# Mamba-2 and latent attention on one core: where the first maxima, the output weight's low halves and the last low halves are computed

## The chip, the cores and the metric

The kernel runs on one core of a Trainium2 chip. The metric is the device time of one execution in microseconds (us); three executions were timed, and one execution was recorded by the hardware profiler. The engines are TensorE (PE in the profile, with its weight loads as PEld), VectorE (DVE), ScalarE (ACT), GpSimd (POOL) and SyncE (SP), which here only issues DMAs. The granted clock is the share of its full speed that TensorE was allowed in a stretch of the trace.

## The reference

Two layers over 2048 tokens of 1024 channels: a Mamba-2 mixer, then multi-head latent attention with 16 heads. The change lies in the second layer:

```python
def causal_block_attention(q_nope, q_rope, k_nope, k_rope, v):
    scale = (QK_NOPE + QK_ROPE) ** -0.5          # 64 + 32
    ...
    s = (q_nope . k_nope + q_rope . k_rope) * scale
    p = softmax(where(mask, s, -inf))
    return p @ v

def mla_mixer(h, k_nope, k_rope, v, cos, sin, w_in, g_q, w_uq, w_out):
    cq, gate = split(h @ w_in, [384])
    q = (rms_norm(cq, g_q) @ w_uq).reshape(..., 16, 64 + 32)
    ...
    o = causal_block_attention(q_nope, q_rope, k_nope, k_rope, v)
    o = o.reshape(..., 1024) * silu(gate)
    return o @ w_out
```

The result is `h + mla_mixer(...)`, followed by a last RMS norm. Every product is made to nearly float32 precision: an operand is split into a high half and a low half (high = the value rounded to a short type, low = value minus high), and three products high·high, high·low, low·high are added in PSUM.

## The kernel before, in words

**Stages.** Tokens go in four blocks of TB = 512. After the Mamba-2 layer, `mla` runs over the blocks b = 0 to 3: the latent key and value, the query's latent, then two gate sweeps (`mla_gate(b, 0)` and `mla_gate(b, 1)`), each of which multiplies eight 128-channel pieces of the input with four 128-column pieces of the gate weight, in eight steps of twelve products (L84 to L86, three for each pair of halves). Between the steps `mla` calls a few items of `mla_up`: keys (groups 0 and 1), values (2 and 3), the query's rotary part (6) and the query (4 and 5). The driver asks for two items a step in sweep 0 and one a step in sweep 1. An item's result is split by ScalarE and VectorE (`pair16`, L115 and L116) and written to DRAM by GpSimd's DMA queue. A gate result is emptied from its PSUM bank by ScalarE (tanh, L1081) and VectorE (product, L1082).

**PSUM.** Eight banks of 128x512 float32: four under the tag "mm" and four under "tr". Gate sweep 0 holds "mm" and sweep 1 holds "tr"; key and value items use "tr", query items "mm". In attention, six banks are called "s" (scores and maxima) and two "o".

**Attention.** `heads` treats 64 jobs (16 heads by four query blocks). For each job it first needs the maximum of each row of scores. This is made in chunks of up to 512 keys: a product (L1239) and a VectorE reduction (L1242), whose second operand, the `fence`, masks the keys that a query does not see. When a job's last chunk is done, the maxima are copied to float16 by ScalarE (L1248), the remainder is subtracted by GpSimd (L1249), VectorE transposes both (L1251), and a DMA through `m_d` puts them into two extra rows of the query tile. Job n's scores can then be made with the maximum already subtracted: `scores` (L1258) handles a *duo*, two tiles of 128 keys by 512 queries, with three products for each tile (and a mask on the diagonal), ScalarE's exponential (L1276) and copy to the high half (L1281). The low half of the probabilities (`lows`, L1291, tile `PTs`) is a subtraction by GpSimd in two pieces of 512 columns for full duos, and by VectorE for diagonal duos, in one piece, one duo later. `values` (L1306 to L1308) multiplies a duo's probabilities with the values some duos later. There are 320 duos.

**What sets the order.** Each engine works through its own queue in the order in which the program is written; PE's order in attention is written by hand. The list `due` says how far the maxima must have come at each duo; `some(...)` makes chunks up to a point, four times in a duo. Ahead of the first duo, `some(due[0])` makes 31 chunks: the 24 of jobs 0 to 2 and 7 of job 3. In some 16 duos at the end no maxima are left to make.

**The output weight.** While attention ends, `back` has already begun in the queues: its `weights(k)` splits eight 128x1024 pieces of the output weight, the high half by ScalarE (L1408), the low half by GpSimd (L1409). Pieces 2 to 5 go to tiles `W` (some 70 us ahead of attention's end), pieces 0, 1 into the first key tile `K0`, and pieces 6, 7 into the second, `K1`, which is free only when attention is done. The back stage multiplies by pieces 0 to 7 in turn.

**Tiles.** `xT` holds the eight pieces of a block's input (high and low half side by side), later the query tiles of attention; `K0` and `K1` hold keys and values of two heads, with room left behind them.

## Time and profile before

| | |
|---|---|
| median of 3 runs | 2934.28 us (2931.23 to 2935.17) |
| the profiled execution | 2936.12 us, of which its span is 2934.3 us |
| mean granted clock of TensorE | 0.987 |
| TensorE busy | 97% of the span |
| VectorE, ScalarE, GpSimd busy | 71%, 62%, 30% |
| DMA | 441.30 MB, mean 150 GB/s |

The profile page and the trace's views give times in us from the start of the span. A row of a timeline reads: start, duration, engine, line of the kernel, operation, output <- inputs, shapes and types, a count if several lie side by side, and in brackets the idle time of that engine just before, with what ended it. A row of a group gives the number of instructions, their busy time, and the mean in ns of one. The last block's gate sweeps and projections end at 1997 us (first chunk of maxima); attention goes from there to about 2747; the back stage follows.

### The profile page before, as it was taken

The numbers are of one execution on the slowest core, as the hardware profiler recorded it, in microseconds if no ns is written. First come the engines' busy times: TensorE is split into PE (matmuls) and PEld (weight loads), VectorE is DVE, ScalarE is ACT, GpSimd is POOL, SyncE is SP. The second block draws the span as 40 slices with busy tenths as digits, with TensorE's granted clock in tenths as the row PEclk, the third lists the DMA queues.
The fourth block names the chain that finished last, engine by engine and source line by source line (L and its number), as shares of the span: only waits on it lengthen the run. The fifth ranks groups of instructions, "written<-read, shape, count | busy, mean of one in ns | idle before, by whom it ended". The sixth has DMA issues, their size and how long they took to land. (4 is left out here: it accounts for less than half of the span.)

```text
span 2934.3 us, 58650 instructions
## 1 busy us (share of the span) xinstructions
PE 2844.8 (97%) x21582; PEld 1670.0 (57%) x21582; DVE 2096.4 (71%) x5050; ACT 1830.4 (62%) x3976; POOL 874.8 (30%) x993
## 2 busy tenths in 40 slices
PE   7899999999999999999999999998999999998998
PEld 3456556555555555554565545544666666665787
DVE  6789887887777778788775554346777777776354
ACT  8777655666666666556553433234888888887512
POOL 0212221221212212122211121222665665666300
PEclk9999999999999999999999999998999999999999
DMA  8765535445474445636446655561212223222452
GB/s 285 253 203 190 170 119 208 156 141 168 134 243 141 139 160 192 225 126 202 137 152 217 200 186 177 183 200 54 69 49 70 63 52 73 66 66 84 161 198 108
DMA packets 244755, 441.30 MB, mean 150 GB/s; under 512 B 69842, under 2 KB 111506, under 8 KB 243028
## 3 DMA queue, kind: packets, MB, share of 16 engines
q1 hardware_dynamic: 233332, 401.64, 43.0%
q0 software_dynamic: 11136, 35.92, 3.4%
q8 instruction: 169, 2.77, 0.4%
q14 instruction: 118, 0.97, 0.1%
HBM read 332.73 MB, written 104.73 MB: 149 GB/s over the span
## 5 line engine op out<-in xcount | busy, mean ns | idle before, releaser
L1291 POOL TENSOR_TENSOR PTs<-x,PTs 128x512 f16<-128x512 f32 x384 | 437.5, 1163 | 248.3 <-ACT PTs L1281 163.9
L1276 ACT ACTIVATE x<-s 128x512 f32<-128x512 f32 (+3 forms) x640 | 327.4, 525 | 56.4 <-PE s L1272 36.2
L84 PE MATMUL mm<-xT,wsp 128*128 128x512 f16 x800 | 305.8, 382 | 8.3 <-ACT wsp L115 6.1
L85 PE MATMUL mm<-xT,wsp 128*128 128x512 f16 x800 | 304.9, 381 | 0.0
L86 PE MATMUL mm<-xT,wsp 128*128 128x512 f16 x800 | 304.1, 381 | 0.0
L1281 ACT ACTIVATE PTs<-x 128x1024 f16<-128x1024 f32 (+1 forms) x320 | 297.1, 928 | 9.4
L1242 DVE CUSTOM_DVE_ANT_0 junk<-s,fence,mx 128x512 bf16<-128x512 f32 (+3 forms) x384 | 249.5, 650 | 46.9 <-PE s L1239 4.1
L1308 PE MATMUL o<-K,PTs 128*128 128x65 f16 x2176 | 263.2, 193 | 7.6 <-POOL PTs L1291 7.0
L1306 PE MATMUL o<-K,PTs 128*128 128x64 f16 x2176 | 264.6, 192 | 0.0
L1307 PE MATMUL o<-K,PTs 128*128 128x65 f16 x2176 | 264.3, 194 | 0.0
L802 POOL TENSOR_TENSOR Xp<-Xw,Xp 128x512 fp32r<-128x512 f32 x64 | 89.5, 1398 | 501.0 <-ACT Xp L801 300.8
L1239 PE MATMUL s<-K,xT 96*128 96x512 f16 (+3 forms) x640 | 225.8, 356 | 12.4 <-DVE mx L1242 10.8
L1306 PEld LDWEIGHTS <-PTs 128*128 128x128 f16 x2176 | 204.9, 97 | 52.3 <-issue 4.7
L85 PE MATMUL mm<-wsp,xT 128*128 128x512 f16 (+1 forms) x640 | 231.0, 361 | 3.2 <-DVE wsp L116 3.2
L84 PE MATMUL mm<-wsp,xT 128*128 128x512 f16 (+1 forms) x640 | 231.0, 362 | 2.9 <-ACT craw L606 2.6
L1307 PEld LDWEIGHTS <-PTs 128*128 128x128 f16 x2176 | 203.1, 97 | 53.5 <-issue 1.1
L612 DVE SCALAR_TENSOR_TENSOR cacc<-craw,pack,cacc 128x512 f32<-128x512 f32 x288 | 216.3, 779 | 23.9 <-ACT cacc L610 23.0
L86 PE MATMUL mm<-wsp,xT 128*128 128x512 f16 (+1 forms) x640 | 231.3, 362 | 0.0
L1270 PE MATMUL s<-xT,K 98*128 98x512 f16 (+3 forms) x640 | 224.9, 351 | 4.0 <-DVE mx L1242 4.0
L1271 PE MATMUL s<-xT,K 96*128 96x512 f16 (+3 forms) x640 | 224.6, 351 | 0.0
L1272 PE MATMUL s<-xT,K 96*128 96x512 f16 (+3 forms) x640 | 222.8, 348 | 0.0
L1308 PEld LDWEIGHTS <-PTs 128*128 128x128 f16 x2176 | 201.9, 98 | 8.6 <-POOL PTs L1291 8.1
(458 smaller groups left out, 7219.3 us busy)
## 6 DMA issues: line engine op xcount, KB each, us to landing
wsp<-wi_d SPq DMA_DIRECT2D x96, 512.0 KB
big<-cumT SPq DMA_DIRECT2D x64, 512.0 KB
wraw<-in_ssm_w_out_dram SPq DMA_DIRECT2D x96, 256.0 KB
wi_d<-wsp SPq DMA_DIRECT2D x32, 512.0 KB
wsp<-wo_d SPq DMA_DIRECT2D x32, 512.0 KB
wsp<-wu_d SPq DMA_DIRECT2D x28, 512.0 KB
hx<-in_ssm_w_in_dram SPq DMA_DIRECT2D x48, 256.0 KB
wraw<-in_ssm_w_in_dram SPq DMA_DIRECT2D x48, 256.0 KB
```

Of the source, the lines that this page charges most:

```text
L84: mm(out, l_hi, r_hi, start=start, stop=False)
L85: mm(out, l_hi, r_lo, start=False, stop=False)
L86: mm(out, l_lo, r_hi, start=False, stop=stop)
L1239: mm(s[:, :w], Q[0:96, 0, qs], K[0:96, 0, c0:c0 + w], start=True, stop=True)
L1242: v.tensor_tensor_reduce(junk[:, :w], s[:, :w], fence[:, at:at + w], -1.0 / MSCALE, peak[n][:, i - 1, j:j + 1] if i else 3.0e38, ALU.add, ...
L1270: mm(s, K[0:98, 0, ks], Q[0:98, 0, c], start=True, stop=False)
L1276: act(o, s, AF.Exp)
L1281: act(u[:, 0, at:end], x[:, at:end], AF.Copy)
L1291: engine.tensor_tensor(u[:, 1, a:b], x[:, a:b], u[:, 0, a:b], ALU.subtract)
L1306: mm(o[:, 0:64], hi, V[:, k, 0:64], start=k == 0 and j == 0, stop=False, skip_group_check=True)
L1307: mm(o[:, 0:65], hi, V[:, k, 64:129], start=False, stop=False, skip_group_check=True)
L1308: mm(o[:, 0:65], lo, V[:, k, 64:129], start=False, stop=k == 4 * qb + j, skip_group_check=True)
```

## The change

Three things move. First, the chunks of jobs 0, 1 and 2 are made by a new generator, `first_maxima`, three after each step of the last block's second gate sweep, in the "mm" banks. For that, all items of `mla_up` of the last block are issued with the first sweep (three a step, the rest at its end); the first two query tiles get a place behind the keys and values in `K0` and `K1`, filled as soon as blocks 0 and 1 are known; a third, of the high half alone, gets an "xs" tile. `heads` builds a fence of its own again, and its loop starts with 24 chunks made, and without the call ahead of the first duo. Second, `weights(k)` has VectorE make the low half. Third, once all chunks are made, a duo's low half is cut at column 512: VectorE makes the columns below, GpSimd those above, both at once.

The core of the diff (helpers `cuts`, `raise_fence`, `peaks`, `turn_peaks` and `rows` hold the code that stood in `heads`):

```diff
@@ mla @@
-                go(up, 2)
+                go(up, 3 if last else 2)
...
             go(cq)
+            if last:
+                go(up)
...
-            after = iter(()) if last else self.prep(NB + b + 1, None, "mm", 1)
+            after = self.first_maxima() if last else self.prep(NB + b + 1, None, "mm", 1)
             for n in range(8):
                 go(main, 1)
                 go(up, 1)
-                if not last:
-                    go(after, 1)
-                elif n == 2:
+                go(after, 3 if last else 1)
+                if last and n == 0:
                     self.load_vq()
@@ open_heads, load_vq, load_q @@
+            at = 2 * T + T // P * 130
+            Q = self.quer[0, i] = kv[i][0:98, at:at + 2 * TB].rearrange("p (s t) -> p s t", s=2)
+            self.fill_q(Q, 0, i)
...
         self.load_k(0, NB - 1, NB)
-        self.load_q(0, 0)
         self.load_v(0)
-        self.load_q(0, 1)
...
+    def first_maxima(self):
+        nc = self.nc
+        late, misc = (self.t(self.sp, "xs", [P, 2, TB], BF16, bufs=8) for _ in range(2))
+        Q2, junk = late[0:96, 0].bitcast(F16), late[:, 1]
+        misc = misc.rearrange("p s t -> p (s t)")
+        fence = self.raise_fence(misc[:, 0:TB + P])
...
+        nc.gpsimd.memset(turned, 0.0)
+        ts = slice(2 * TB, 3 * TB)
+        nc.sync.dma_start(Q2[0:64], self.qn_d[0:64, 0, ts])
+        nc.sync.dma_start(Q2[64:80], self.q1_d[0:16, 0, ts])
+        nc.sync.dma_start(Q2[80:96], self.q2_d[0:16, 0, ts])
+        K = self.keys[0]
+        for n in range(3):
+            Q = Q2 if n == 2 else self.quer[0, n][:, 0]
+            for j in range(4):
+                parts = self.cuts(n, j)
+                for i, (c0, w) in enumerate(parts):
+                    s = self.t(self.pp, "mm", [P, TB], bufs=4)
+                    self.peaks(s, Q[:, j * P:(j + 1) * P], K[:, 0, c0:c0 + w], fence, junk, peak[:, n], i, j,
+                               i == len(parts) - 1)
+                    if j < 3 or i < len(parts) - 1:
+                        yield
+            self.turn_peaks(n, peak[:, n, n], turned[:, 32 * n:32 * n + 32], rT[:, 32 * n:32 * n + 32])
+            if n < 2:
+                self.rows(n, self.quer[0, n])
+            yield
@@ heads @@
-        fence = self.t(sp, "fence", [P, TB + P], BF16, bufs=1)
-        nc.gpsimd.memset(fence[:, :TB], -LIFT)
-        nc.gpsimd.tensor_scalar(fence[:, TB:], self.mk, -LIFT, None, ALU.add)
...
+        fence = self.raise_fence(self.t(sp, "fence", [P, TB + P], BF16, bufs=1))
+        for n in range(2, 5):
+            self.load_q(n // NB, n % NB)
+        self.rows(2, quer[0, 2])
...
-            if kb < 4 * qb:
+            if made == len(chunks):
+                lows(u, x, at, TB, v)
+                lows(u, x, TB, end, nc.gpsimd)
+            elif kb < 4 * qb:
                 lows(u, x, at, end, nc.gpsimd)
             else:
                 fresh.append((u, x, at, end, v))
...
-            cut = [at, TB, end] if engine is nc.gpsimd else [at, end]
+            cut = [at, TB, end] if engine is nc.gpsimd and at < TB else [at, end]
...
-        step, later, held, fresh, made = [0], [], [], [], 0
+        step, later, held, fresh, made = [0], [], [], [], ends[2]
...
-        some(due[0])
@@ back, weights @@
-                nc.gpsimd.tensor_tensor(lo, self.wraw[k], hi.bitcast(F32), ALU.subtract)
+                v.tensor_tensor(lo, self.wraw[k], hi.bitcast(F32), ALU.subtract)
```

How the instructions stand on the engines, at three places. On PE, at the end of the last sweep: before, the last product of a query item (into `mm`) is followed by the first chunk's product (`s`, keys times the query tile `xT`):

```order
L86 MATMUL mm_21633<-yT_21103,wsp_21436 128x512
L1239 LDWEIGHTS xT_21454
L1239 MATMUL s_21680<-K_3813_20590,xT_21454 128x128
L1239 LDWEIGHTS xT_21454
L1239 MATMUL s_21684<-K_3813_20590,xT_21454 128x256
L1239 LDWEIGHTS xT_21454
```

Now the same chunks (L1213, into `mm` banks, query and keys both in the key tile) stand between the first two steps' products of the sweep (`tr`):

```order
L85 MATMUL tr_21511<-xT_20319,Xd_21519 128x512
L86 LDWEIGHTS Xd_21519
L86 MATMUL tr_21511<-xT_20319,Xd_21519 128x512
L1213 LDWEIGHTS K_3813_20590
L1213 MATMUL mm_21538<-K_3813_20590 128x128
L1213 LDWEIGHTS K_3813_20590
L1213 MATMUL mm_21541<-K_3813_20590 128x256
L1213 LDWEIGHTS K_3813_20590
L1213 MATMUL mm_21544<-K_3813_20590 128x384
L84 LDWEIGHTS y_21514
L84 MATMUL tr_21512<-xT_20261,y_21514 128x512
```

What moved: the chunks, from behind the sweep into it, three a step. On GpSimd, at the start of attention, before: the last stores of query items, three memsets, the fence, and then the subtractions for jobs 0 to 2:

```order
L1104 DMA qn_d<-Xp_21643 256x1x512
L1198 MEMSET nm_4003_21663 128x32
L1198 MEMSET nm_4004_21664 128x32
L1198 MEMSET nm_4005_21665 128x32
L1201 MEMSET fence_21669 128x512
L1202 TENSOR_SCALAR fence_21669<-mk 128x128
L1249 TENSOR_TENSOR nm_4003_21663<-mx_21675,nm_4003_21663 128x4
L1249 TENSOR_TENSOR nm_4004_21664<-mx_21703,nm_4004_21664 128x4
```

Now the three subtractions (L1223, in an `xs` tile) come first, and `heads`' memsets and its fence (which the 25th chunk reads) behind them:

```order
L1105 DMA qn_d<-big_21506 256x1x512
L1223 TENSOR_TENSOR xs_21531<-xs_21531 128x4 x3
L1271 MEMSET nm_4027_21757 128x32
L1271 MEMSET nm_4028_21758 128x32
L1271 MEMSET nm_4029_21759 128x32
L1206 MEMSET fence_21763 128x512
L1207 TENSOR_SCALAR fence_21763<-mk 128x128
L1350 TENSOR_TENSOR PTs_21852<-x_21851,PTs_21852 128x512 x2
```

What moved: the subtractions, ahead of the fence. On GpSimd some 70 us ahead of attention's end, before: three of the weight pieces (`W`) between the low halves of probabilities (`PTs`) and a subtraction for maxima (`nm`):

```order
L1291 TENSOR_TENSOR PTs_35556<-x_35555,PTs_35556 128x512 x2
L1409 TENSOR_TENSOR W_37173<-wr_35496,W_37173 128x2x512
L1291 TENSOR_TENSOR PTs_35612<-x_35611,PTs_35612 128x512 x2
L1409 TENSOR_TENSOR W_37209<-wr_37067,W_37209 128x2x512
L1291 TENSOR_TENSOR PTs_35652<-x_35651,PTs_35652 128x512 x2
L1249 TENSOR_TENSOR nm_4004_21664<-mx_35593,nm_4004_21664 128x4
L1409 TENSOR_TENSOR W_37243<-wr_37102,W_37243 128x2x512
```

Now the same pieces stand on VectorE, between the reductions of chunks (L1215), a head's result (`Op`) and a gating product of the back stage (`xT`, L1482):

```order
L1384 TENSOR_TENSOR Op_35621<-o_35431,ri_35619 128x4x64
L1467 TENSOR_TENSOR W_37155<-wr_35472,W_37155 128x2x512
L1215 ISA junk_35634,mx_35569<-s_35635,fence_21763 128x512
L1215 ISA mx_35569 128x1
L1482 SCALAR_TENSOR_TENSOR xT_37086<-xT_37086,us_37036 128x512
L1215 ISA junk_35659,mx_35569<-s_35660,fence_21763,mx_35569 128x384
L1215 ISA mx_35569 128x1
L1467 TENSOR_TENSOR W_37191<-wr_37049,W_37191 128x2x512
```

What moved: the weight pieces, from GpSimd's queue into VectorE's.

## The prediction

> **What bounds the kernel now.** I read the page first, then the windows around the places that the change touches, then the engines' timelines there.

> ```profile
> span 2934.3 us, 58650 instructions
> PE 2844.8 (97%) x21582; PEld 1670.0 (57%) x21582; DVE 2096.4 (71%) x5050; ACT 1830.4 (62%) x3976; POOL 874.8 (30%) x993
> PEclk9999999999999999999999999998999999999999
> ```

> TensorE (PE) is busy for 97% of the span, and its products are the same before and after. So only time in which PE stands idle, or runs under a lowered clock, can be won. The clock row has one dip, in slice 28, where attention starts. The windows (columns: time and length, busy us of PE, its weight loads, DVE, ACT, POOL, then granted clock, DMA share, GB/s) show the dips:

> ```profile
> 1976.00:1997.00 21.00, 21.00 (x99) 9.56 (x98) 7.25 (x10) 6.22 (x10) 3.38 (x5) 1.00 0.43 146
> 2000.00:2010.00 10.00, 6.01 (x12) 1.25 (x12) 7.37 (x26) 0.41 (x2) 1.19 (x4) 0.50 0.08 27
> 2010.00:2020.00 10.00, 6.49 (x13) 1.25 (x12) 8.38 (x26) 0.20 (x1) 0.38 (x2) 0.50 0.01 2
> 2020.00:2030.00 10.00, 9.42 (x51) 4.65 (x50) 8.01 (x24) 5.38 (x10) 0.02 (x1) 0.64 0.09 23
> 2660.00:2670.00 10.00, 7.39 (x89) 4.49 (x87) 8.70 (x25) 8.64 (x14) 8.10 (x7) 1.00 0.49 164
> 2670.00:2680.00 10.00, 6.04 (x63) 3.44 (x64) 4.64 (x9) 6.54 (x12) 10.00 (x8) 0.79 0.30 101
> 2680.00:2690.00 10.00, 10.00 (x84) 5.40 (x83) 7.94 (x22) 5.68 (x8) 5.50 (x6) 0.70 0.15 54
> 2735.00:2740.00 5.00, 5.00 (x74) 3.46 (x73) 0.00 (x0) 4.94 (x7) 5.00 (x5) 1.00 0.02 3
> ```

> In the last gate sweep (first row) PE is full and VectorE (DVE) only a third busy. Behind it, for some 24 us, VectorE sets the pace with the first maxima, and PE's clock falls to half. Around 2670 us GpSimd (POOL) is full; at the end of attention (last row) VectorE idles while GpSimd and ScalarE (ACT) are full. The change's three parts aim at these three places.

> **Part a, the first maxima in the gate sweep.** PE's timeline (start, duration) gives the sweep's step, its end, the first scores and the clock's return:

> ```profile
> 1988.69 0.38 PE L84 MATMUL tr<-xT,st 128*128 128x512 f16 x1
> 1991.28 0.38 PE L84 MATMUL mm<-yT,wsp 128*128 128x512 f16 x1
> 1997.11 0.22 PE L1239 MATMUL s<-K,xT 96*128 96x128 f16 x1
> 2021.25 0.59 PE L1270 MATMUL s<-xT,K 98*128 98x512 f16 x1 [0.32 <-DVE mx L1242]
> 2027.17 0.41 PE L1271 MATMUL s<-xT,K 96*128 96x512 f16 x1
> ```

> Twelve products of 512 columns, one step, take 1991.28 − 1988.69 = 2.59 us, 0.216 each; eight steps take 20.7. All up-projections now stand ahead of this sweep. PE was full up to 1997.11 and does the same work, so the sweep starts at 1997.11 − 20.7 = 1976.4, plus 0.9 for two query projections that wait in sweep 0 for a PSUM bank still being emptied: 1977.3. (Emptying takes 1.8: a product's 0.38 and a bit, tanh and its VectorE product at 0.69 each, rows below. A query projection has nine products, 1.94 us, so one of them between two uses of a bank covers it. By the order that stands for nearly all; two stand closer, and I estimate 0.2 and 0.7.) The 24 chunks laced in, blocks 0, 1 and 2 of head 0, hold 1280 + 3328 + 5376 = 9984 columns: 9984/512 × 0.216 = 4.2 us of PE. So PE leaves the sweep at 1977.3 + 20.7 + 4.2 = 2002.2, instead of reaching the first scores at 2021.25.

> VectorE does not follow that fast. ACT's tanh and VectorE's rows (brackets: idle time before it, and what ended it):

> ```profile
> 1944.21 0.69 ACT L1081 ACTIVATE xs<-mm,mdown 128x512 f32<-128x512 f32 x1 [0.70 <-PE mm L86]
> ```

> ```profile
> 1944.93 0.69 DVE L1082 SCALAR_TENSOR_TENSOR xs<-xs,mm 128x512 f32<-128x512 f32 x1 [0.69 <-ACT xs L1081]
> 2001.02 0.29 DVE L1242 CUSTOM_DVE_ANT_0 junk<-s,fence 128x128 bf16<-128x128 f32 x1 [2.24 <-POOL fence L1202]
> 2018.69 0.75 DVE L1242 CUSTOM_DVE_ANT_0 junk<-s,fence,mx 128x512 bf16<-128x512 f32 x1
> 2019.59 0.69 DVE L1242 CUSTOM_DVE_ANT_0 junk<-s,fence 128x512 bf16<-128x512 f32 x1
> ```

> The row at 2019.59 is the 25th chunk; the 24 ahead of it took 2019.59 − 2001.02 = 18.57 us. In the sweep, with four gate evacuations of 0.69 among them, VectorE needs about 21.3 us if nothing stops it; three chunks a step, in steps that are now 2.59 + 0.5 long, spread them over 25, and the last ones, the widest, come at the sweep's end together with the evacuations. I set the last chunk's end at 1977.3 + 28.9 = 2006.2: PE's 24.9, one emptying of 1.8, and three chunks of 0.75. Then the 25th chunk waits for a new fence, which GpSimd makes behind the last job's subtraction and three memsets; queued behind it on VectorE are the seven other chunks and, on PE, every score that needs their banks. The prices:

> ```profile
> 1999.64 0.37 POOL L1198 MEMSET nm<- 128x32 f16 x3
> 1999.81 0.65 POOL L1201 MEMSET fence<- 128x512 bf16 x1
> 2000.32 0.67 POOL L1202 TENSOR_SCALAR fence<-mk 128x128 bf16<-128x128 bf16 x1
> ```

> From 1999.64 to 2000.99 is 1.35, which I set whole behind the last chunk, so the 25th chunk starts at 2007.6 instead of 2019.59: 12.0 earlier. The rest of the program hangs on this: seven chunks remain, as before, but now beside duo 0's scores. PE, ahead of it by 5 us, runs out of banks, and its clock will dip once more. Before, the dense work from 2021.25 to 2027.17 ran at half clock and lost 3.0; I take half of that off, 1.5. **a = 10.5** (7 if the whole sweep is stretched by VectorE's lateness, 19 if PE's own front, 2002.2 against 2021.25, decides).

> The moved step's DMAs cost nothing by this order: value, key and query loads of head 0 are issued on SP in the sweep, with DMA shares of 0.43 and 0.08 in the first two windows; the query loads of blocks 3 and 4 stand on SP behind xT buffers that PE frees in the sweep. If the query tile of block 2 came late, its 13 chunks, from step 4 on, would wait; its three loads have four steps, over 10 us.

> **Part b, the output weight's low halves.** PE's gaps, VectorE's and GpSimd's rows at the first four of them:

> ```profile
> 2670.10 0.20 PE L1308 MATMUL o<-K,PTs 128*128 128x65 f16 x1 [0.94 <-POOL PTs L1291]
> 2671.22 0.20 PE L1308 MATMUL o<-K,PTs 128*128 128x65 f16 x1 [0.35 <-POOL PTs L1291]
> 2674.64 0.20 PE L1308 MATMUL o<-K,PTs 128*128 128x65 f16 x1 [2.02 <-POOL PTs L1291]
> 2676.77 0.59 PE L1239 MATMUL s<-K,xT 96*128 96x512 f16 x1 [0.94 <-DVE mx L1242]
> 2679.84 0.59 PE L1239 MATMUL s<-K,xT 96*128 96x512 f16 x1 [0.56 <-DVE mx L1242]
> ```

> ```profile
> 2675.90 0.21 DVE L1251 STREAM_TRANSPOSE rT<-nm 128x32 f16<-128x32 f16 x1 [5.36 <-POOL nm L1249]
> 2676.63 2.49 DVE L1291 TENSOR_TENSOR PTs<-x,PTs 128x896 f16<-128x896 f32 x1
> ```

> ```profile
> 2675.82 2.35 POOL L1409 TENSOR_TENSOR W<-wr,W 128x1024 fp32r<-128x1024 f32 x1
> 2678.12 3.43 POOL L1291 TENSOR_TENSOR PTs<-x,PTs 128x512 f16<-128x512 f32 x2
> ```

> A weight's low half holds GpSimd for 2.35 us, the probabilities' low halves queue behind it, and VectorE idles 5.36 for a 0.2 us subtraction on GpSimd. PE waits 0.94 + 0.35 + 2.02 = 3.31 for GpSimd and 0.94 + 0.56 = 1.50 for VectorE that was held; the lowered clock (0.70 of a full PE in the last window) costs 3.0, and about 1.0 in the one before. At stake: 8.8. Added on VectorE, per weight: by its own rows of this operation,

> ```profile
> L1291 DVE TENSOR_TENSOR PTs<-x,PTs 128x896 f16<-128x896 f32 x64 | 72.7, 1136 | 16.8 <-ACT PTs L1281 16.7
> L1291 DVE TENSOR_TENSOR PTs<-x,PTs 128x384 f16<-128x384 f32 x64 | 35.5, 555 | 0.0
> ```

> (1136 − 555)/512 = 1.13 ns a column, so 1.28 us for 1024 columns, and up to 2.6 beside GpSimd (2.49 for 896 at 2676.63). I take 1.7: nearer the grouped row, since only some fall beside GpSimd. Three weights in this stretch put 5.1 in front of maxima that PE waits for. 8.8 − 5.1 = 3.7: **b = 4** (0 to 8). The two weights in the key tile's place at the end cost PE nothing: the back stage needs them last, for its seventh and eighth products of a block, and VectorE has their time: they are hidden by the first six, or would cost 2 × 1.7.

> **Part c, the last low halves by two engines.** From the page and PE's gaps:

> ```profile
> L1291 POOL TENSOR_TENSOR PTs<-x,PTs 128x512 f16<-128x512 f32 x384 | 437.5, 1163 | 248.3 <-ACT PTs L1281 163.9
> ```

> ```profile
> 2713.41 0.23 PE L1308 MATMUL o<-K,PTs 128*128 128x65 f16 x1 [2.22 <-POOL PTs L1291]
> 2742.37 0.20 PE L1308 MATMUL o<-K,PTs 128*128 128x65 f16 x1 [0.56 <-POOL PTs L1291]
> 2743.48 0.20 PE L1308 MATMUL o<-K,PTs 128*128 128x65 f16 x1 [0.58 <-POOL PTs L1291]
> 2744.43 0.20 PE L1308 MATMUL o<-K,PTs 128*128 128x65 f16 x1 [0.41 <-DVE PTs L1291]
> ```

> A pair costs GpSimd 2 × 1.163; halved, GpSimd has 1.16 a duo and VectorE 0.7. The gaps sum to 3.8. In the row 2735:2740 PE is full and ACT at 4.94 of 5.00, so nothing is to be won between them; two weights on VectorE (1.7 each) stand ahead of two last chunks. **c = 3** (1 to 5).

> [...] The row at 2676.63 took 2.49 us beside GpSimd's weight, which ended at 2678.17, 0.95 before it. [...]

> **Sum.** 10.5 + 4 + 3 = 17.5. The profiled execution took 2936.12 (span 2934.3 and 1.8 around it) and would take 2918.6; the median of the runs lies 1.84 below it, at 2934.28, so I forecast 2934.28 − 17.5 = 2916.8, or **2917 us**.

> **Rivals.**

> A: PE's front decides. VectorE catches up in duos 0 to 3, since only 7 chunks are owed, and a = 19; b 7, c 4.5. Then 2934.28 − 30.5 = **2904**. For it: behind 2020 VectorE is busy 8.01 of 10, at a half clock. Against: PE's banks are handed on by VectorE, and its row of maxima has no gap.

> B: the two engines, working at once, hold each other up for the whole of an instruction, so b and c give 0: 2934.28 − 10.5 = **2924**. For it: the 2.49 at 2676.63 (1.136 in the mean) and the pair of 3.43 behind it (2 × 1.163 in the mean). Against: not every instruction meets another.

> C, the slower side: PSUM in sweep 0. The twelve query-side projections share four banks with the gate's accumulators and now follow them at once. If each waits for a whole emptying and its hand-over, some 2.0 us, that is 24 us, and 2934.28 − 17.5 + 24 makes **2941**. It decides from 17.5/12 = 1.5 us a projection; at 1.0 each the time, 2929, is within 0.2%. For it: no spare bank stands between them. Against: four banks in turn, and the 1.94 of each projection covers the bank of the next.

> **Chances.** Forecast 0.52, A 0.17, B 0.17, C 0.14 (0.06 slower, 0.08 partial, within 0.2%). So faster 0.86, same 0.08, slower 0.06; 0.2%, 5.9 us, is about what a measurement of this kernel can tell from no change. The range, **2903 to 2927**, runs from A to a = 7 with b and c at 0, and leaves out C and a little more.

> **What would show it.** Right: the first scores (now L1326) near 2002, the 25th chunk near 2008, a clock dip between them; PE's gaps for GpSimd near 2660 gone, weights on VectorE at 1.3 to 2.6; no gap over 1 us for low halves at the end. Wrong: PE gaps for banks in the two sweeps (C); low halves of about 2.5 on both engines (B); scores right behind the sweep at full clock (A). A late block-2 query tile, or maxima waiting for keys that SP issues late, would undo a.

## The result and the profile after

The changed kernel takes **2915.02 us** (median of 4, 2911.01 to 2917.16) against 2933.98 (median of 4, 2931.23 to 2935.17) in the same set: ratio 0.9935, interval 0.9918 to 0.9952. A second set, timed later beside other runs, gave 2912.8 (5 runs) against 2935.87 (9 runs): ratio 0.9922, interval 0.991 to 0.9935. So 19.0 and 23.1 us are gained; the forecast was 2917, 17.5 less than before.

The page of the kernel after, first part and the clock row:

```profile
span 2909.2 us, 58684 instructions
PE 2833.6 (97%) x21582; PEld 1668.1 (57%) x21582; DVE 2109.2 (73%) x5068; ACT 1828.1 (63%) x3976; POOL 860.4 (30%) x984
PEclk9999999999999999999999999999999999999999
```

TensorE's busy time fell by 11.2 us (2844.8 to 2833.6) with the same 21582 products: for the most part that is the clock, since a product at half clock counts longer: with 512 columns, the next starts 0.43 us later at 2011.42, in the dip, and 0.22 later at 2013.61, behind it (in the half-speed stretches of attention TensorE was busy 31.21 us before and 9.31 after; half of the difference is 10.95). The dip in slice 28 is gone from this coarse row. In windows (columns as before) it is still there, but short:

```profile
1976.00:1997.00 21.00, 21.00 (x103) 9.74 (x102) 12.95 (x43) 1.78 (x4) 1.09 (x3) 1.00 0.27 79
1997.00:2010.00 13.00, 10.56 (x43) 4.64 (x42) 11.14 (x30) 5.28 (x10) 1.34 (x6) 0.74 0.36 110
2010.00:2020.00 10.00, 10.00 (x107) 6.02 (x106) 7.58 (x24) 7.37 (x12) 4.54 (x4) 0.82 0.01 2
2020.00:2030.00 10.00, 10.00 (x131) 6.37 (x130) 8.07 (x29) 8.46 (x14) 7.89 (x9) 1.00 0.03 5
2660.00:2670.00 10.00, 8.31 (x95) 4.76 (x93) 9.11 (x26) 6.53 (x9) 8.35 (x8) 1.00 0.16 55
2670.00:2680.00 10.00, 10.00 (x160) 7.32 (x159) 7.67 (x22) 9.08 (x16) 5.66 (x6) 1.00 0.02 3
```

The last gate sweep is still full on TensorE, and VectorE's busy time in the same 21 us rose from 7.25 to 12.95: the maxima fit into the gaps. By 2010 TensorE is full again; before, it stood at 6 of 10 until 2020.

**A common clock for the two traces.** This execution is 2.26 us ahead before the change begins: VectorE's last gate product of block 2 starts at 1875.75 before and at

```profile
1873.49 0.69 DVE L1083 SCALAR_TENSOR_TENSOR xs<-xs,tr 128x512 f32<-128x512 f32 x1
2900.49 0.69 DVE L1497 TENSOR_TENSOR h<-h,tr 128x512 f32<-128x512 f32 x1 [3.38 <-PE tr L86]
```

after; the second row is the last residual sum, the end of the back stage. From the first to the second are 1027.0 us here and 1050.13 before. All times in the tables below are counted from that gate product, so what comes ahead of the change drops out. Marks between are ScalarE's exponentials, counted from 0 to 639 (L1276 before, L1332 after), and the first piece of the last value product. A difference between two marks prices one place of the program.

| from the gate product, us | before | after | gain |
|---|---|---|---|
| VectorE done with the 24th chunk | 143.69 | 128.60 | 15.1 |
| VectorE starts the 25th chunk | 143.85 | 129.78 | 14.1 |
| TensorE starts the first scores | 145.50 | 125.90 | 19.6 |
| exponential 100 | 257.96 | 243.33 | 14.6 |
| exponential 540 | 744.14 | 729.50 | 14.6 |
| exponential 610 | 834.16 | 814.62 | 19.5 |
| last value product | 869.45 | 846.21 | 23.2 |
| last residual sum | 1050.13 | 1027.00 | 23.1 |

So 14.6 are won at the start of attention, 4.9 where the output weight's pieces W are made, 3.7 between there and attention's end, nothing behind. VectorE at the first of these places:

```profile
2001.33 0.75 DVE L1215 CUSTOM_DVE_ANT_0 xs<-mm,xs 128x512 bf16<-128x512 f32 x1
...
2002.64 0.21 DVE L1224 STREAM_TRANSPOSE xs<-xs 128x32 f16<-128x32 f16 x1 [0.55 <-POOL xs L1223]
2003.27 0.69 DVE L1215 CUSTOM_DVE_ANT_0 junk<-s,fence 128x512 bf16<-128x512 f32 x1 [0.41 <-POOL fence L1206]
```

The 24th chunk, then 0.55 of waiting for GpSimd's subtraction, then 0.41 for the new fence, then the 25th. TensorE there:

```profile
1999.39 0.38 PE L1326 MATMUL s<-K 98*128 98x512 f16 x1
...
2001.24 0.38 PE L1213 MATMUL s<-K,xT 96*128 96x512 f16 x1 [0.98 <-DVE xs L1215]
...
2002.14 0.59 PE L1213 MATMUL s<-K,xT 96*128 96x512 f16 x2 [0.53 <-DVE xs L1215]
...
2004.02 1.49 PE L1213 MATMUL s<-K,xT 96*128 96x512 f16 x3 [0.67 <-DVE mx L1215]
```

It reaches the first scores right behind the sweep, and then waits three times for a bank that VectorE still reads. The last row's three products take 1.49 where two took 0.59 just before: the clock has fallen, at 2003.29, just ahead of the third wait, for 10.24 us.

At the second place, TensorE's gaps (eight for VectorE, 4.53 in all) and VectorE's rows, three weight pieces among them:

```profile
2644.60 0.22 PE L1213 MATMUL s<-K,xT 96*128 96x128 f16 x1 [0.83 <-DVE mx L1215]
2645.44 0.38 PE L1326 MATMUL s<-xT,K 98*128 98x512 f16 x1 [0.23 <-DVE mx L1215]
...
2646.96 0.38 PE L1326 MATMUL s<-xT,K 98*128 98x512 f16 x1 [0.50 <-DVE mx L1215]
...
2652.98 0.38 PE L1213 MATMUL s<-K,xT 96*128 96x512 f16 x1 [0.43 <-DVE mx L1215]
...
2655.15 0.38 PE L1213 MATMUL s<-K,xT 96*128 96x512 f16 x1 [0.19 <-DVE mx L1215]
...
2658.24 0.38 PE L1326 MATMUL s<-xT,K 98*128 98x512 f16 x1 [0.73 <-DVE mx L1215]
...
2661.43 0.38 PE L1213 MATMUL s<-K,xT 96*128 96x512 f16 x1 [0.74 <-DVE mx L1215]
2663.33 0.38 PE L1213 MATMUL s<-K,xT 96*128 96x512 f16 x1 [0.88 <-DVE mx L1215]
```

```profile
2643.22 0.85 DVE L1482 SCALAR_TENSOR_TENSOR xT<-xT,us 128x512 f32<-128x512 f32 x1 [2.08 <-issue]
...
2649.15 1.54 DVE L1467 TENSOR_TENSOR W<-wr,W 128x1024 fp32r<-128x1024 f32 x1
...
2652.85 1.64 DVE L1467 TENSOR_TENSOR W<-wr,W 128x1024 fp32r<-128x1024 f32 x1
...
2658.24 1.18 DVE L1467 TENSOR_TENSOR W<-wr,W 128x1024 fp32r<-128x1024 f32 x1
```

No gap for GpSimd is left beside the W pieces; all are for VectorE, and none is over 0.9. The first row of VectorE is a gating product of the back stage, 2.08 late, which the first three gaps follow; before, three gaps of the same kind came ahead of those that the prediction lists:

```profile
2661.13 0.22 PE L1239 MATMUL s<-K,xT 96*128 96x128 f16 x1 [1.03 <-DVE mx L1242]
...
2661.97 0.38 PE L1270 MATMUL s<-xT,K 98*128 98x512 f16 x1 [0.23 <-DVE mx L1242]
...
2663.49 0.38 PE L1270 MATMUL s<-xT,K 98*128 98x512 f16 x1 [0.50 <-DVE mx L1242]
```

With 0.94 and 0.56 they make 3.26.

At the third place, the sharing (VectorE's 512 columns, then GpSimd's), and TensorE's gaps for low halves. The first two of these gaps stand where 0.35 and 2.22 stood before:

```profile
2697.61 0.69 DVE L1350 TENSOR_TENSOR PTs<-x,PTs 128x512 f16<-128x512 f32 x1 [1.29 <-ACT PTs L1337]
```

```profile
2697.71 1.61 POOL L1350 TENSOR_TENSOR PTs<-x,PTs 128x512 f16<-128x512 f32 x1 [0.94 <-PE o L1367]
```

```profile
2687.96 0.20 PE L1367 MATMUL o<-K,PTs 128*128 128x65 f16 x1 [0.32 <-POOL PTs L1350]
2690.05 0.20 PE L1367 MATMUL o<-K,PTs 128*128 128x65 f16 x1 [0.90 <-POOL PTs L1350]
...
2718.50 0.20 PE L1367 MATMUL o<-K,PTs 128*128 128x65 f16 x1 [0.55 <-DVE PTs L1350]
2719.27 0.20 PE L1367 MATMUL o<-K,PTs 128*128 128x65 f16 x1 [0.23 <-POOL PTs L1350]
```

### The profile page after: what moved, and what is told of

Same layout as the page of the kernel before. It is cut to its first block, busy times and chain, and to the rows that moved or that the text cites. A ratio compares the mean times of both kernels' runs of the same rounds, so it can differ in the third digit from the quotient of the medians.

```text
span 2909.2 us, 58684 instructions
## 1 busy us (share of the span) xinstructions
PE 2833.6 (97%) x21582; PEld 1668.1 (57%) x21582; DVE 2109.2 (73%) x5068; ACT 1828.1 (63%) x3976; POOL 860.4 (30%) x984
## 4 chain that ended last, share of the span: by engine, by line
PE 43%; issue 3%; DVE 3%; ACT 2%; DMA 1%; POOL 1%; DVEq 0%; SPq 0%; POOLq 0%; ACTq 0%
PE s L1326 4%; PE s L1327 4%; PE mm L84 4%; PE s L1328 4%; PE mm L86 4%; PE mm L85 4%; PE s L1213 4%; PE tr L84 3%; PE tr L86 3%; PE tr L85 3%; PE o L1366 2%; PE o L1367 2%; PE o L1365 2%; DVE junk L1215 1%; PE s L1394 0%
## 5 line engine op out<-in xcount | busy, mean ns | idle before, releaser
L1350 POOL TENSOR_TENSOR PTs<-x,PTs 128x512 f16<-128x512 f32 (+1 forms) x380 | 439.0, 1178 | 263.5 <-ACT PTs L1337 174.5
L1332 ACT ACTIVATE x<-s 128x512 f32<-128x512 f32 (+3 forms) x640 | 326.7, 524 | 50.3 <-PE s L1328 31.6
L84 PE MATMUL mm<-xT,wsp 128*128 128x512 f16 x800 | 306.6, 383 | 7.9 <-ACT wsp L115 5.6
L86 PE MATMUL mm<-xT,wsp 128*128 128x512 f16 x800 | 305.3, 382 | 0.0
L1215 DVE CUSTOM_DVE_ANT_0 junk<-s,fence,mx 128x512 bf16<-128x512 f32 (+1 forms) x372 | 242.1, 651 | 43.7 <-PE s L1213 3.0
L84 PE MATMUL mm<-wsp,xT 128*128 128x512 f16 (+1 forms) x640 | 231.4, 362 | 3.2 <-ACT craw L606 2.9
L86 PE MATMUL mm<-wsp,xT 128*128 128x512 f16 (+1 forms) x640 | 231.6, 362 | 0.0
L1326 PE MATMUL s<-xT,K 98*128 98x512 f16 (+1 forms) x628 | 218.5, 348 | 4.1 <-DVE mx L1215 3.7
L1213 PE MATMUL s<-K,xT 96*128 96x512 f16 (+1 forms) x616 | 213.9, 350 | 5.6 <-DVE mx L1215 4.1
L1327 PE MATMUL s<-xT,K 96*128 96x512 f16 (+1 forms) x628 | 218.4, 348 | 0.0
L1328 PE MATMUL s<-xT,K 96*128 96x512 f16 (+1 forms) x628 | 217.0, 345 | 0.0
```

The costliest lines, as they stand in the source:

```text
L84: mm(out, l_hi, r_hi, start=start, stop=False)
L86: mm(out, l_lo, r_hi, start=False, stop=stop)
L1213: self.nc.tensor.matmul(s[:, :w], Q[0:96], K[0:96], start=True, stop=True)
L1326: mm(s, K[0:98, 0, ks], Q[0:98, 0, c], start=True, stop=False)
L1327: mm(s, K[0:96, 0, ks], Q[0:96, 1, c], start=False, stop=False)
L1328: mm(s, K[0:96, 1, ks], Q[0:96, 0, c], start=False, stop=kb < 4 * qb)
```

## The experiments

Every run here has one profile; the table gives differences of marks, the lengths of the half-speed stretches (behind the sweep / from 100 us ahead of the last value product to 5 us behind it) and the medians.

| run | exp. 540 | 540 to 610 | 610 to last value product | back stage | half clock, us | median us | ratio to before (interval) |
|---|---|---|---|---|---|---|---|
| before | 744.14 | 90.02 | 35.30 | 180.67 | 27.3 / 10.2, 3.4 | | |
| after | 729.50 | 85.13 | 31.58 | 180.79 | 10.2 / none | 2915.02 | 0.9935 (0.9918 to 0.9952) |
| after_again | 730.07 | 85.48 | 31.63 | 181.59 | 10.2 / none | 2912.80 | 0.9922 (0.991 to 0.9935) |
| a_only | 729.11 | 89.69 | 36.59 | 180.60 | 10.2 / 10.2, 6.8 | 2922.33 | 0.9952 (0.9937 to 0.9967) |
| no_split | 729.33 | 84.70 | 32.30 | 183.37 | 10.2 / 6.8 | 2914.40 | 0.9929 (0.9914 to 0.9943) |
| no_b | 730.32 | 91.17 | 35.84 | 182.28 | 10.2 / 10.2, 6.8, 3.4 | 2918.11 | 0.9935 (0.992 to 0.9951) |
| k0_pool | 730.42 | 86.24 | 34.68 | 181.22 | 10.2 / 3.4 | 2916.16 | 0.9937 (0.9923 to 0.9952) |
| tail_dve | 730.59 | 85.50 | 31.53 | 182.24 | 13.7 / 3.4 | 2913.43 | 0.992 (0.9906 to 0.9934) |
| fence_kept | 725.89 | 84.88 | 31.60 | 183.11 | none / 3.4 | 2910.85 | 0.9916 (0.9899 to 0.9932) |
| front_loaded | 727.09 | 84.96 | 31.61 | 182.28 | none / 3.4 | 2912.06 | 0.9922 (0.9905 to 0.9938) |
| fill_waits | 727.84 | 86.10 | 31.61 | 180.91 | none / none | 2915.73 | 0.9937 (0.992 to 0.9954) |
| both | 725.26 | 84.77 | 31.62 | 181.84 | none / none | 2907.51 | 0.9901 (0.9887 to 0.9914) |

Between exponential 540 and 610 the runs differ also by something that none of the edits is about. ScalarE splits the first W piece there and waits for the DMA that brings it, 1.37 to 3.38 us; the exponentials queue behind it, and TensorE waits for them: 1.67 in `no_b`, 1.32 in `k0_pool`, 1.27 in `fill_waits`, 0.68 in `tail_dve`, and with the same kernel 0.30 in `after` and 0.65 in `after_again`; not at all in the others. The row of `no_b`:

```profile
2633.16 1.06 ACT L1466 ACTIVATE W<-wr 128x1024 fp32r<-128x1024 f32 x1 [3.38 <-DMA wr<-in_mla_w_out_dram]
```

**Parts a, b and c apart.** `a_only` undoes b and c:

```diff
-                v.tensor_tensor(lo, self.wraw[k], hi.bitcast(F32), ALU.subtract)
+                nc.gpsimd.tensor_tensor(lo, self.wraw[k], hi.bitcast(F32), ALU.subtract)
...
-            if made == len(chunks):
-                lows(u, x, at, TB, v)
-                lows(u, x, TB, end, nc.gpsimd)
-            elif kb < 4 * qb:
+            if kb < 4 * qb:
```

> Part a alone: the first maxima stay in the gate sweep, the weight's low halves go back to GpSimd, the last low halves are not shared. Measured on the stretch from VectorE's last gate product of block 2 to its last residual sum, which took 1050.12 us before and 1026.99 with the whole change. Theory (the parts add up, and a is what ScalarE's exponentials show in mid-attention, 14.6): 1035.5, about 14.6 under before. Rival (the pace behind duo 0 is set by the clock's dip, which is not the change's doing): anything between 1038 and 1043. In the trace the GpSimd waits of 2.02 and 2.22 are back.

Measured: 1035.99, so 14.1 for part a; the theory holds, the rival is out. Both GpSimd waits are back, 2.01 and 2.23 against 2.02 and 2.22 before, some 16 us earlier in the span. TensorE, then GpSimd ahead of the second wait, of `a_only`:

```profile
2659.02 0.20 PE L1364 MATMUL o<-K,PTs 128*128 128x65 f16 x1 [2.01 <-POOL PTs L1347]
...
2697.49 0.24 PE L1364 MATMUL o<-K,PTs 128*128 128x65 f16 x1 [2.23 <-POOL PTs L1347]
```

```profile
2689.41 2.36 POOL L1464 TENSOR_TENSOR K<-wr,K 128x1024 fp32r<-128x1024 f32 x1 [7.46 <-ACT K L1463]
2691.73 2.28 POOL L1347 TENSOR_TENSOR PTs<-x,PTs 128x512 f16<-128x512 f32 x2
2693.97 2.36 POOL L1464 TENSOR_TENSOR K<-wr,K 128x1024 fp32r<-128x1024 f32 x1
2696.28 2.27 POOL L1347 TENSOR_TENSOR PTs<-x,PTs 128x512 f16<-128x512 f32 x2
```

The low halves for which TensorE waits 2.23 (2696.28) stand on GpSimd behind a weight piece for the first key tile (2693.97). That points to part b, not to part c.

`no_split` undoes only the second hunk above.

> Parts a and b, without c. Same stretch. Theory (b is worth 4.8 with VectorE's share of the weight pieces, c 3.7): 1030.7. Rival (the two engines exclude each other, so b gives nothing and c everything, or the other way round): 1035.5 if b is nothing, 1027 if c is nothing.

Measured: 1029.70, of which the back stage has 183.37 (a half-speed stretch of 6.8 us at its start), so the whole number misleads. By the marks: from `a_only` to `no_split` b takes 89.69 − 84.70 = 5.0 at the W pieces and 36.59 − 32.30 = 4.3 at the two key-tile pieces, **9.3 in all**; from `no_split` to the whole change c takes 32.30 − 31.6 = **0.7**. The theory had 8.5 for the two and the shares wrong; of the rival, the half in which c is nothing comes nearer, though not for its reason. (Against the whole change, `no_b` below gives 6.0 and 4.3 for b; 1.4 of the 6.0 is the longer wait for ScalarE that stands under the table.) Of the 9.3, the waits are the smaller part: TensorE's gaps over 0.15 us, from exponential 540 to the last value product, sum to 10.4 in `a_only` and 7.9 in `no_split`. The other 6.8 are put down to the clock: `a_only` has 10.24 and 6.83 us at half speed there, `no_split` none.

`no_b` undoes only the first hunk, to see whether c is worth more without b.

> Parts a and c, without b: the weight's low halves go back to GpSimd. The runs so far: with a alone the last product of attention starts 855.39 into the stretch, with a and b 846.33, with all three 846.21. Theory (the GpSimd waits before the end, 0.35 and 2.23 in a alone, come from the two weight pieces on GpSimd, and c has its worth only while these are there): c takes 1.5 to 4 off, the last product starts between 851.4 and 853.9. Rival (c is worth nothing with or without b, since ScalarE and TensorE are full there): 855.4 within 0.5. Second rival (c's forecast 3 was right, and in the whole change it is lost to VectorE's weight pieces): 852.4 here, and the GpSimd wait of 2.2 is gone.

Measured: the last value product at 857.33, later than with a alone. Up to exponential 610, where c has hardly begun, this run is already 2.7 behind `a_only`, so the last value product's time can't decide; 1.7 of TensorE's waiting for ScalarE lies in between. From 610 on it takes 35.84 against 36.59: c is worth 0.75 there, and the wait of 2.23 is still there. So c is worth 0.7 with b and without, a little over the first rival's 0.5; theory and second rival fall.

`k0_pool` gives GpSimd the pieces 0 and 1 alone:

```diff
-                v.tensor_tensor(lo, self.wraw[k], hi.bitcast(F32), ALU.subtract)
+                (nc.gpsimd if k < 2 else v).tensor_tensor(lo, self.wraw[k], hi.bitcast(F32), ALU.subtract)
```

> The whole change, but the two weight pieces for the first key tile (0 and 1) go back to GpSimd; the four ahead of them stay on VectorE. Theory (the GpSimd wait of 2.2 in the tail, which the prediction put to part c, belongs to these two pieces): from exponential 610 to the last product of attention 35.8, as in the run without b, instead of 31.6; exponential 610 itself at 815 as with the whole change. Rival (c takes that wait away by itself, once the other pieces are off GpSimd): 31.6 to 33.

Measured: 34.68, so 3.1 for these two pieces (4.3 in the pair above, which had a half-speed stretch of 6.8 here where this one has 3.4), and exponential 610 at 816.66, 1.1 to 2.0 later than with the whole change, of which 0.7 to 1.0 is the longer wait for ScalarE. TensorE of `k0_pool`:

```profile
2692.03 0.20 PE L1367 MATMUL o<-K,PTs 128*128 128x65 f16 x1 [0.35 <-POOL PTs L1350]
2695.46 0.20 PE L1367 MATMUL o<-K,PTs 128*128 128x65 f16 x1 [2.23 <-POOL PTs L1350]
```

The same two waits, 0.35 and 2.2, with c in place; with these pieces on VectorE they are 0.32 and 0.90, and no less without c (0.33 and 0.90 in `no_split`). So 1.3 of the 2.2 belong to these pieces, and 0.9 to neither part. The rival is out; the size is 1.1 under what the theory said.

**All of a last low half on VectorE.** `tail_dve`:

```diff
-                lows(u, x, at, TB, v)
-                lows(u, x, TB, end, nc.gpsimd)
+                lows(u, x, at, end, v)
```

> The whole change, but once all maxima are made VectorE makes the whole low half of a duo, and GpSimd none. In the shared form the trace shows VectorE's 512 columns at 0.69 and GpSimd's 512 begun beside them at 1.61 to 1.68, where an undisturbed one takes 1.16: GpSimd waits for VectorE. Theory (the engines take turns at these instructions): 1024 columns on VectorE take 1.2 to 1.3, so the low half is ready 0.3 to 0.5 sooner than in the shared form, and the last product of attention starts 0.2 to 0.6 before 846.21. Rival (they only slow each other in part, and sharing is the faster way): it starts 0.3 or more after 846.21.

Measured: the last value product at 847.61, 1.4 later. The rival had 0.3 or more, but 1.1 of these are there at exponential 540 already, with a longer dip behind the sweep, and the rest by 610. From 610 on, where the edit acts, it takes 31.53 against 31.58 and 31.63. So neither account holds. The instruction did what the theory said:

```profile
2701.28 1.23 DVE L1349 TENSOR_TENSOR PTs<-x,PTs 128x1024 f16<-128x1024 f32 x1 [0.84 <-ACT PTs L1337]
```

1.23 for 1024 columns, where the shared form is done after about 1.7. But TensorE waits for few of them: at the end 0.89 for one, where it waits 0.55 and 0.23 in the shared form. A low half that is ready 0.5 sooner is worth 0.1 at most here.

**What is left behind the sweep.** `after_again` is the changed kernel once more.

> The whole change, unaltered, profiled a second time and timed beside the variants. Theory (the half-speed dip of 10.24 us behind the sweep belongs to TensorE's waits there, 0.98 + 0.53 + 0.67 us, which part a leaves; three profiled runs with these waits had it): the dip of 10.24 us is there again, the stretch from VectorE's last gate product of block 2 to its last residual sum within 1 of 1027 unless attention's end has a dip too (then up to 3 more). Rival (whether a dip falls there is chance): no dip there, and exponential 540 comes 3 us sooner than the 729.5 of before.

Measured: the dip of 10.24 again, the stretch 1028.77, which is 1.8 more (0.8 of it the back stage's) and so just outside the 1 that was allowed; exponential 540 at 730.07. `fence_kept` makes the fence and the zeroed tiles once, ahead of the gate sweeps:

```diff
@@ open_heads @@
+        at += 2 * TB
+        self.fence = self.raise_fence(kv[1][:, at:at + TB + P].bitcast(BF16))
+        self.turned3 = kv[1][:, at + TB + P:at + TB + P + 96]
+        nc.gpsimd.memset(self.turned3, 0.0)
...
@@ heads @@
-        turned = [self.t(sp, f"nm{i}", [P, 32], F16, bufs=1) for i in range(3)]
-        for u in turned:
-            nc.gpsimd.memset(u, 0.0)
-        fence = self.raise_fence(self.t(sp, "fence", [P, TB + P], BF16, bufs=1))
+        turned = [self.turned3[:, 32 * i:32 * i + 32] for i in range(3)]
+        fence = self.fence
```

> The whole change, but the fence and the zeroed tiles for the transposes are made once, before the gate sweeps, in free columns of the second key tile, and attention uses them again. Theory (the 25th chunk waits for GpSimd's fence, 1.2 us from the end of the 24th, and VectorE has no gap behind it): the stretch falls from 1026.99 to 1026.0, by 1.0, and by up to 3 more if the clock's half-speed dip, now 10.24 us long, shortens. Rival (TensorE at half clock sets the pace there, not VectorE): unchanged within 0.3, the dip 10.24 as before.

Measured: the 25th chunk starts at 129.29, 0.49 sooner (not 1.0: the 0.55 for GpSimd's subtraction stays), there is no dip (part of that may be chance: see the last section), exponential 540 comes 3.2 to 4.7 sooner than in the runs with the dip; the stretch, 1025.48, keeps only 1.5 of that against `after`, since the back stage took 183.11. `front_loaded` has another rhythm:

```diff
-                go(after, 3 if last else 1)
+                go(after, (4 if n < 4 else 2) if last else 1)
```

> The whole change, but four chunks after each of the first four sweep steps and two after each of the last four, instead of three. Theory (TensorE waits 0.98 + 0.53 + 0.67 us behind the sweep because VectorE still has the last chunks and gate products, and that idling is what brings the clock down): these waits shrink to under 1 us in all, the dip goes or shortens, the stretch falls by 2 to 6 us. Rival (VectorE's sum of work sets the pace whatever the order): VectorE's 25th chunk starts no more than 0.5 earlier, stretch within 0.5 of 1026.99.

Measured: the 24th chunk done at 127.9 instead of 128.6, the 25th started 0.70 sooner, TensorE's first three waits 0.89, 0.67 and 0.31 instead of 0.98, 0.53 and 0.67 (1.87, not the under 1 that the theory said), no dip, exponential 540 at 727.09.

`fill_waits` adds useless products in TensorE's waits (they write a bank that nobody reads):

```diff
+        spare = self.t(self.ap, "o", [P, TB], bufs=2)
...
             while cols[made] < due:
+                for _ in range({24: 4, 25: 2, 28: 3}.get(made, 0)):
+                    mm(spare, keys[0][0:96, 0, 0:P], keys[0][0:96, 0, 0:TB], start=True, stop=True)
                 maxima(*chunks[made])
```

> The whole change, and nine products of 512 columns whose result nobody reads, put on TensorE where it waits behind the sweep: four ahead of the 25th chunk, two ahead of the 26th, three ahead of the 29th (0.216 us each at full clock, beside waits of 0.98, 0.53 and 0.67). They add work and shorten no wait of another engine. Theory (idle TensorE, and not VectorE's lateness, brings the half-speed dip there): the dip goes, although the 25th chunk starts no sooner on VectorE (129.8 into the stretch); exponential 540 comes 2.5 to 4 before the 729.8 that six runs with the dip show in the mean. Rival (the dip comes with the change of stage, or the fence's wait, whatever TensorE does): the dip of 10.24 is there, exponential 540 at 729.8 or up to 1 later.

Measured: the 25th chunk at 129.78, exactly as before the edit, and no dip; windows of `fill_waits` (its own times, 4.7 later than in `after`):

```profile
2000.00:2005.00 5.00, 5.00 (x26) 2.30 (x25) 4.75 (x12) 2.06 (x3) 0.00 (x0) 1.00 0.50 169
2005.00:2010.00 5.00, 4.23 (x22) 1.92 (x21) 3.60 (x11) 2.13 (x4) 1.34 (x6) 1.00 0.47 157
2010.00:2015.00 5.00, 4.05 (x31) 1.97 (x30) 4.54 (x13) 2.96 (x6) 0.00 (x0) 1.00 0.04 9
```

The granted clock stays 1.00 throughout. Exponential 540 comes at 727.84, 2.1 before the mean of seven runs with the dip (729.9). So TensorE's idling there brings the dip, as the theory said, with one profile to show it; the 2.1 is a little less than it said, and what is left after the useless products have taken their time. The rival is out. The median, 2915.73, is no lower than the changed kernel's: in the profile, 1.0 of the 2.1 is lost again to a longer wait for ScalarE (1.27 against 0.30).

**A version that beats both.** `both` joins the edits of `fence_kept` and `front_loaded`.

> The two variants together: the fence kept in the second key tile, and four chunks after each of the first four sweep steps, two after the others. Theory (each takes away a different piece of the wait behind the sweep): the 24th chunk ends 127.9 into the stretch as with the front-loaded sweep, the 25th starts by 128.6 (129.08 and 129.29 with one of them), no dip behind the sweep, exponential 540 at 725.3 (725.89 and 727.09 with one of them). Rival (what is left is TensorE waiting for the banks of the last chunks, and the two gains are the same one): exponential 540 at 725.9 or later.

Measured: 24th chunk done at 127.91, 25th started at 128.60, no dip, exponential 540 at 725.26, and a median of **2907.51 us**, ratio 0.9901 (0.9887 to 0.9914), 5.3 under the changed kernel in the same set. As the theory said; the second edit adds 0.6 to the first. The windows of `both`:

```profile
1997.00:2010.00 13.00, 10.63 (x80) 5.45 (x79) 11.04 (x32) 8.50 (x15) 2.67 (x4) 1.00 0.28 88
```

TensorE still idles 2.4 of these 13 us, spread in smaller pieces, at full clock.

## Why the prediction was right, point by point

**Sign and time.** 2915 lies 2 us from the 2917 that was forecast, and that is partly luck. The parts behind it were less exact: by the marks 14.3 for a (mean of seven runs with the dip against before, 744.14 − 729.9), 9.3 for b, 0.7 for c, where 10.5, 4 and 3 stood. That makes 24.3, 6.8 more than the forecast: a and b were set too low, c too high. The profile gained 23.1 from the gate product on, the second set of medians 23.1, and only the first set 19.0; why that one is less isn't shown.

**Part a.** TensorE's own front was right: first scores at 125.90, where 2002.2 − 1875.75 = 126.45 was forecast, and the sweep was stretched only by its 4.2 us of chunks: TensorE has no gap of over 0.06 us in the 90 us ahead of the first scores. Rival C did not happen: the sweep began at 103.51 − 2.59 = 100.92 (its first chunk's product stands at 1977.0 in the trace, one step behind it), 0.3 behind the ideal 100.65, where 0.9 was allowed. Nor did rival A: the front's 19.6 had shrunk to 14.6 by exponential 100, and TensorE's waits behind the sweep are for VectorE's reductions. Two terms of the sum were mis-sized. VectorE's end of the 24th chunk was set a whole emptying and three chunks behind TensorE (130.45); it was 128.60, so VectorE stood 2.70 behind TensorE's front and not 4.05. And 1.5 was taken off for the clock, though the kernel before had a dip there too, a longer one: the gain at the 25th chunk, 14.1, arrives at exponential 540 as 14.3. The fence's wait (1.35 forecast, 1.18 measured from the 24th chunk's end to the 25th) was right.

**Part b.** The step that failed is "three weights in this stretch put 5.1 in front of maxima that PE waits for". The pieces cost VectorE 1.54, 1.64 and 1.18, near the 1.7, but they stood where VectorE had been idle for GpSimd: TensorE's gaps for VectorE grew from 3.26 to 4.53, by 1.3 and not 5.1, while the gaps for GpSimd, 3.31, went and with them the dip of 10.24. That is 5.0 net at the W pieces, the larger half of it by the clock. The other 4.3 (3.1 by `k0_pool`) come from the first key tile's pieces, which the prediction left out of b. What they cost stood in the wrong part:

**Part c.** The wait of 2.22 at 2713.41 was counted for c, and c takes none of it: it is 2.23 in `no_b` and `k0_pool`, which have c, and 0.90 in `no_split`, which does not. 1.3 of it belonged to b: GpSimd was late because of the weight pieces for the first key tile, which stand in its queue ahead of those low halves. A half-speed stretch of 3.41 came behind it, and that went too. The 0.90 is left. What is c's own is the last three gaps, 0.56 + 0.58 + 0.41 = 1.55, of which 0.55 + 0.23 are left: 0.8, the measured 0.7. The row at 2735, with ScalarE at 4.94 of 5.00, had said so: nothing between is to be won.

**Rival B.** The two engines do hold each other up: at 2697.61 VectorE's 512 columns took 0.69, no longer than by the prediction's rows (0.555 for 384 columns and 1.13 ns for each of 128 more make 0.70), and GpSimd's, begun 0.10 later, 1.61 instead of 1.16, so 0.45 of the 0.59 in which they met was lost. Held up for the whole of it, as the rival has it, GpSimd would have lost 0.59. The rival's conclusion, that b and c would then be worth nothing, was wrong by 10 us: VectorE does 1024 columns in 1.18 to 1.64 where GpSimd takes 2.35, so a moved piece is done 0.7 to 1.2 sooner, and it clears GpSimd's queue.

**The back stage** was forecast at no change. Its one length before is 180.67; the eleven profiles behind lie between 180.60 and 183.37, 181.84 in the mean. With one profile of before, whether the change costs anything there stays open: in `no_split` a half-speed stretch of 6.8 at its start is part of it, in `fence_kept` TensorE waits for the operand of the next block:

```profile
2764.44 0.47 PE L84 MATMUL mm<-K,oT 128*128 128x512 f32 x1 [1.47 <-ACT oT L107]
```

## What to carry to other kernels

Work that one engine does ahead of a stage, while the main engine waits, can be laced into the stage before if that engine is idle there and a bank is free; what is won is then read at that engine's own end, not at the main engine's front. Before a wait is credited to the edit that touches the instruction waited for, look at what stands ahead of that instruction in its queue: here 1.3 of a gap of 2.2 us for low halves were the price of weight pieces. Look also at the granted clock behind a gap: of the 9.3 us of part b, some 6.8 are put down to TensorE at half speed. And price an instruction that is moved to a busier engine at the place where that engine was waiting, not at its full duration.

## What the runs showed of the hardware

```profile
1999.88:2003.29 3.41, 1.90 (x11) 0.88 (x10) 2.30 (x9) 0.69 (x2) 0.88 (x6) 1.00 0.64 202
...
2003.49:2006.90 3.41, 1.98 (x10) 0.93 (x10) 2.16 (x8) 2.13 (x4) 1.34 (x6) 1.00 0.37 118
...
1999.12:2002.53 3.41, 2.36 (x11) 0.97 (x10) 3.27 (x9) 0.74 (x2) 0.00 (x0) 1.00 0.66 229
2002.53:2005.95 3.42, 2.29 (x13) 1.18 (x13) 2.58 (x8) 2.13 (x4) 0.20 (x1) 1.00 0.42 117
```

In `after` the waits of 0.98 and 0.53 lie in one window, TensorE is busy for 1.90 of it, and the clock falls at its end; the third wait, of 0.67, begins 0.06 behind the fall. In all seven profiles of the changed kernel and its variants that have the dip behind the sweep, the window ahead of it was busy for 0.56 to 0.58, in the kernel before for 0.51. `fence_kept` has the same first two waits, but a border of the grid, 2.3 behind the first scores, parts them. In `k0_pool` the border lies at the same place, and the second window was low enough, by waits of 0.68 and 0.31 where `fence_kept` has one of 0.53. So the edit did its part; a window that holds its first two waits whole would be as low as the one of `after`, and no run shows that case. In all twelve traces there are 98 falls, and TensorE was busy for at most 0.58 of the window ahead of each; but 46 windows as low as that were not followed by a fall. So a low window came ahead of every fall here and is not enough for one; what else decides stays open.

The dip of 10.24 cost 2.1 us by `fill_waits`, and in `fence_kept` 4.0 were gained where its earlier start explains 0.5. At the granted 0.50, a TensorE with nothing else to wait for would have lost half of 10.24, 5.12 by estimate: the products that it slowed stood partly beside VectorE's work. In `after` the window ahead of the dip was not idle (1.90 of 3.41), and the half clock lasted three windows, in which TensorE was busy for 2.75, 3.15 and 3.41 us.

**Spread from the same grid.** At attention's end TensorE waits 0.55, 0.23 and 0.73 within 2.8 us in the changed kernel. In `front_loaded` all three fell into one window, which was busy for 1.84 of 3.41, and 3.4 us at half speed followed; in `after` a border of the grid parted them, and the two windows, busy for 2.53 and 2.74, brought none. So here 3.4 us at half speed came or stayed away with where the grid lay, by these two profiles, and from no edit of that place.
